# A hybrid block on one core: other projections beside the recurrence and the attention, and keys and values in seven-product sets

## The chip, the core and the metric

The kernel runs on one core of one Trainium2 chip. Its engines are TensorE (PE in the profile; PEld is its weight load), VectorE (DVE), ScalarE (ACT), GpSimd (POOL) and SyncE (SP). They run at the same time and wait for each other through semaphores. DMAs are issued from SP (weights) and from POOL (most else). The metric is the device time of one execution in microseconds (us), the median of the runs.

## The reference

256 tokens and 256 context tokens of width 2048 go through one block in float32. After a modulated norm, one wide projection `w_in` gives all inputs of an attention branch and of a recurrent branch (HGRN2, both directions, 16 heads of 128). Both are gated, projected and merged.

```python
xn = rmsnorm(h, norm_gain[l]) * (1.0 + scale) + shift
cn = rmsnorm(hc, norm_gain[l]) * (1.0 + scale_c) + shift_c
aq, ak, av, ag, hq, hff, hfb, hi, hg, ma, mb = split_columns(xn @ w_in[l])
caq, cak, cav, cag, chq, chff, chfb, chi, chg, cma, cmb = split_columns(cn @ w_in[l])
...
att_branch = window_attention(q, k, v, k_c, v_c, sink_logits[l]) * jax.nn.silu(ag)
...
o, _, _ = hgrn2_bidir(q_h, v_h, k_f, g_f, k_b, g_b, s_f, s_b)
hg_branch = hgrn_readout(o, hgrn_norm_gain[l], hg)
...
y_a = hg_branch @ w_o_hgrn_l
y_b = att_branch @ w_o_attn_l
y = jax.nn.sigmoid(m_a + b_m[0]) * y_a + jax.nn.sigmoid(m_b + b_m[1]) * y_b
return y @ w_out_l
```

The attention has 16 query heads and 4 key and value heads of 128, a rotary position (rope) on queries and keys, a window over the own tokens, all context tokens, and a sink. Context tokens are needed for keys, values, forget gates and the recurrent values; the other projections are of the own 256 tokens.

## The kernel before

**Numbers in two parts.** A float32 operand is kept as a high part and a low part, both float32r. `wchunk` (L69) loads a weight chunk of 128x1024 values through SP (tile `raw`, four buffers), ScalarE copies the high part (`wh`, L76) and VectorE subtracts it to get the low part (`wl`, L77). Each product is then three matmuls: high by high, low by high, high by low (`mm_high_first`, L87: L91, L92, L94). The activations lie in `xHL`: `xH` and `xL`, 16 blocks of 128 rows by 512 columns, of which columns 0 to 255 are the own tokens and 256 to 511 the context. The context half is called `XH`, `XL` once it is free.

**Projections.** `proj_tok_g` (L99) is a generator: it works through 8 chunks for a tile of 512 output columns, 24 matmuls of 512 columns a chunk for four token tiles and 12 for two, and yields after each chunk with the matmul columns it issued. `proj_col_x_g` (L138) does the same with features on the partitions. `STEP` is 24 x 512 columns. `quad_tok` (L657) computes 512 output columns for all 512 tokens by a seven-product scheme (as Strassen's, with combinations of the weights formed on VectorE and sums of the activations formed once, in `S`), in two halves of the depth, 24 matmuls of 256 columns a product. `quad_col` (L609) is its counterpart for the forget gates.

**Order of the stages.** Modulation and norm; the recurrent values, by `quad_tok` but for the first; the forget gates, by `quad_col`; the recurrence in 8 pairs of heads (`pair`, L766); `part_a` (L1166: recurrent branch times `w_oh`); the attention (`attend`, L1255); `part_b` (L1337: attention branch times `w_oa`); the output projection.

**How work is woven.** In the quad stage, the recurrence and the attention, TensorE's order is the written one (`manual_schedule`); a planner orders the other engines by its own simulation and by priorities, the pairs' and the attention's steps highest, weight splits next, all else after. `pair` yields the number of STEPs of filler that its next step should have behind it; `weave` (L1013) then draws on a filler generator until so much has been issued. The filler is `side_work` (L1097) for `SIDE[n]` yields, then the query projection of the next pair. `with_gates` (L1125) puts a chunk of the modulation gate (w_ada, on VectorE, `gates`) between, once in 3 STEP. `alternate` (L1029) takes one step of `attend` and one of `fill`. Each of the 32 heads by token tiles n has two steps in `attend`: `scores(n)` with the softmax, and `turned(n-2)`, the four transposes of the probabilities, with `values` once in four tiles.

**What fills what.** The side work holds the output gates of the recurrence, six of the eight merge gates, and the projections of keys and values (`attn_keys`, `attn_values`). The attention's filler `fill` holds queries and gates of the head groups 1 to 3 (`group_in`) and two merge gates. The queries and gates of group 0 are woven with the key transposes ahead of the attention, and `part_a` stands alone between recurrence and attention, with up to 16 steps of the modulation gate in it.

**Buffers.** "sm" is a ring of three tiles of 128x512 that all small results share, "bb" one of two. PSUM has four banks for projections (`pj`) and one each under the names `tp`, `o`, `al1`, `al2`. Results that wait for a later stage go to DRAM tiles and back through POOL's queue (`v_dr`, `hg_dr`, `ma_dr`, `mb_dr`, `k_dr`).

Of the kernel before, what the change touches and what calls it, by code (L numbers as in the profile page):

```python
# [14 lines left out]
P = 128  # L15
# [23 lines left out]
def block_kernel(ctx: ExitStack, tc: tile.TileContext, x, c, cx, c_ctx, w_ada, b_ada, norm_gain, w_in,  # L39
# [184 lines left out]
    k_dr = dram.tile([P, 2048], F32, name="k_dr")  # L224
# [309 lines left out]
    with pl("sp", reuse_waits="tile") as sp:  # L534
# [179 lines left out]
        with tc.manual_schedule(engines={mybir.EngineType.PE}):  # L714
# [17 lines left out]
    biases = {}  # L732
# [33 lines left out]
    def pair(g, p, grp, F, banks_q):  # L766
# [140 lines left out]
        yield 1.5  # L907
# [21 lines left out]
        yield 1.5  # L929
# [9 lines left out]
        yield 3.0  # L939
# [14 lines left out]
        yield 1.0  # L954
# [14 lines left out]
        yield 1.0  # L969
# [59 lines left out]
    def alternate(g, filler, n):  # L1029
        for _ in g:  # L1030
            for _ in range(n):
                next(filler, None)
        run(filler)

# [20 lines left out]
    def rope(dst, src, t):  # L1055

        cos = cs[:, K_COS + t * HD: K_COS + (t + 1) * HD].unsqueeze(1).to_broadcast([P, 4, HD])
        dve.tensor_tensor(dst, src.rearrange("p (h d) -> p h d", h=4), cos, op=ALU.mult)
# [6 lines left out]
        tf = tmp.rearrange("p h a s d -> p h (a s d)")  # L1065
# [8 lines left out]
    def attn_keys():  # L1074
        bk = yield from proj_tok_g(w_in, C_K, x_st, range(4))
        for t in range(4):
            kr_ = base.tile([P, 512], F32, tag="sm", name="kr", bufs=3)
            if t < 2:
                rope(kr_.rearrange("p (h d) -> p h d", h=4), bk[t], t)
            else:  # L1080
                act.activation(kr_, bk[t], AF.Copy)
            nc.gpsimd.dma_start(k_dr[:, t * 512: (t + 1) * 512], kr_)

    def attn_values():
        bv = yield from proj_tok_g(w_in, C_V, x_st, range(4))
        for t in range(4):
            rows = slice(8 + 2 * t, 10 + 2 * t)
            split(XH[:, rows, :], XL[:, rows, :], bv[t].rearrange("p (r c) -> p r c", r=2))
# [7 lines left out]

    def side_work():  # L1097
        for step in ((output_gate(1), merge_out(0, 0), output_gate(2)), (attn_keys(),),
                     (merge_out(0, 1), output_gate(3), merge_out(0, 2)),
                     (merge_out(0, 3), merge_out(1, 2), merge_out(1, 3)), (attn_values(),)):  # L1100
            for g in step:
                yield from g
                yield 0

    side = side_work()
    SIDE = (13, 14, 9, 13, 14, 13, 14, 9)

    def inputs(n, res):

        units, F = 0, None  # L1110
        for _ in range(SIDE[n]):
            got = next(side, None)
            if got is None:
                break
            units += got
            if F is None and n < 7 and units >= 4 * STEP:
                F = load_forgets(n + 1)
            yield got
# [17 lines left out]
    def merge_gate(bm, n, row, dst):  # L1136
        bb = biases.pop((row, n), None)
        if bb is None:
            bb = bias_row(row, n)
        for t in range(2):  # L1140
            dve.tensor_tensor(dst[:, t, :], bm[t], bb, op=ALU.add)
            act.activation(dst[:, t, :], dst[:, t, :], AF.Sigmoid)
# [23 lines left out]
    def part_a(n):  # L1166
        by = proj_tok_g(w_oh, n * 512, b_st, range(2))
        for z in range(4):
            take(gate, 1)
            for _ in range(2):  # L1170
                next(by)
        by = result(by)
        for t in range(2):
            dve.tensor_tensor(y[n][:, t, :], by[t], y[n][:, t, :], op=ALU.mult)

    for n in range(4):
        y[n] = hp.tile([P, 2, 512], F32, tag="vc", name="y") if n == 3 else \
            fp.tile([P, 2, 512], F32, tag="F0" if n < 2 else "F1", name="y", bufs=2 if n < 2 else 1)
        nc.gpsimd.dma_start(y[n].rearrange("p t c -> p (t c)"), ma_dr[n])
    for n in range(4):  # L1180
        part_a(n)
# [19 lines left out]
    with tc.manual_schedule(engines={mybir.EngineType.PE}):  # L1201
# [4 lines left out]
        kr = at.tile([P, 4, 4, HD], F32, tag="A", name="kr")  # L1206
        nc.gpsimd.dma_start(kr.rearrange("p t h d -> p (t h d)"), k_dr)

        def keys():
            for z in range(2):  # L1210
                tks = [ps.tile([P, 512], F32, tag=tg, name="tkk") for tg in ("tp", "o")]
                for t in range(2):
                    for j in range(4):
                        pe.transpose(tks[t][:, j * P: (j + 1) * P], kr[:, 2 * z + t, j, :], ident)

                for t in range(2):
                    dst = [X[:, z: 8: 2, t * P: (t + 1) * P] for X in (XH, XL)]
                    split(dst[0], dst[1], tks[t].rearrange("p (j t) -> p j t", j=4))
                yield

        def group_in(j, st):

            bq = yield from proj_tok_g(w_in, C_Q + 512 * j, x_st, range(2))
            def turn_q(t):
                qr = base.tile([P, 4, HD], F32, tag="bb", name="qr", bufs=2)
                rope(qr, bq[t], t)
                yield
                tk = ps.tile([P, 512], F32, tag="o", name="tkq")
                for i in range(4):
                    pe.transpose(tk[:, i * P: (i + 1) * P], qr[:, i, :], ident)  # L1230
                qh, ql = [X[:, t].rearrange("p h t -> p (h t)") for X in st["q"]]
                with tc.high_priority(2 * PRIO):
                    act.activation(qh, tk, AF.Copy, scale=HD ** -0.5)
                    dve.scalar_tensor_tensor(ql, tk, HD ** -0.5, qh.bitcast(F32), op0=ALU.mult, op1=ALU.subtract)

            turning = [turn_q(t) for t in range(2)]
            next(turning[0])
            st["q"] = [at.tile([P, 2, 4, P], F32R, tag=tg, name="qTa") for tg in Q_TAGS[j % 2]]
            st["g"] = gt_tile(j, [P, 4, T], "ga")
            for hf in range(2):  # L1240
                bg = proj_col_x_g(w_in, C_G + 512 * j + 256 * hf)
                for k0 in range(0, KT, 4):
                    next(bg)
                    yield
                    if (hf, k0) == (0, 0):
                        next(turning[1])
                    if hf == 0 and k0 in (4, 12):
                        next(turning[k0 // 8], None)
                for i, b in enumerate(result(bg)):
                    gs = halves_sum(b, "bb", 2)  # L1250
                    gi = st["g"][:, 2 * hf + i, :]
                    act.activation(gi, gs, AF.Sigmoid)
                    dve.tensor_tensor(gi, gi, gs, op=ALU.mult)
# [240 lines left out]
```

## Time and profile before

| | us |
|---|---|
| median of the runs (1612.27 to 1616.04) | 1614.99 |
| the profiled execution | 1614.37 |
| its span | 1612.6 |
| busy TensorE, VectorE, ScalarE, GpSimd | 1579.2, 1152.4, 863.7, 84.8 |
| quad stage, from the recurrent values on | 200 to 573 |
| recurrence | 573 to 1052 |
| `part_a` up to the last of it | to about 1140 |
| attention with its first projections | 1140 to 1440 |

The page is of one execution. Busy times are of instructions, and matmuls overlap, so the start of one matmul to the start of the next tells more than the length of one. A row of windows gives, for a stretch, its length and then busy time and number of instructions of PE, PEld, DVE, ACT and POOL, the granted TensorE clock (1.00 is full), the busy share of the DMA engines and GB/s. A row of waits gives who waited at which line, for whom, the sum in us, how often, and the longest.

### The profile page before, as it was taken

Reading aid. Unit: us, or ns where it says so; the run is one execution under the profiler, and the core shown is the slowest. Engines: PE = TensorE matmul, PEld = TensorE weight load, DVE = VectorE, ACT = ScalarE, POOL = GpSimd, SP = SyncE. Lnnn points to the kernel's source line nnn. Section 1 sums busy time; section 2 is a strip of 40 time slices with the busy share of each in tenths; the row PEclk is TensorE's granted clock in tenths of the full one; section 3 lists DMA queues with packets and bytes.
Section 4 is the critical chain, followed back from the end, with each engine's and each line's share of the span. In section 5 each row is a group of like instructions: output and inputs, shape, how many; then the busy total and the mean of one; then the engine's idle time right before and its main releaser. Section 6 shows DMA issues by size and latency. Waiting matters only on the chain. (4 is left out here: it accounts for less than half of the span.)

```text
span 1612.6 us, 26672 instructions
## 1 busy us (share of the span) xinstructions
PE 1579.2 (98%) x10522; PEld 1336.6 (83%) x10522; DVE 1152.4 (71%) x1703; ACT 863.7 (54%) x1337; POOL 84.8 (5%) x183
## 2 busy tenths in 40 slices
PE   7999999999999999999999999999999999999998
PEld 4567899988888887888888888878888888888887
DVE  4449777788888877876888787556567767756674
ACT  4334443356565565655666666434457677744442
POOL 2000000000000010111111010000000000000000
PEclk9999999999999999999999999999999999999999
DMA  9995434444444486564767766467554445467662
GB/s 364 386 373 170 157 131 131 131 132 131 131 135 140 133 276 217 191 223 158 228 224 240 244 213 205 159 215 249 180 179 144 146 141 164 158 230 235 207 208 80
DMA packets 230013, 312.76 MB, mean 194 GB/s; under 512 B 10080, under 2 KB 145664, under 8 KB 228992
## 3 DMA queue, kind: packets, MB, share of 16 engines
q1 hardware_dynamic: 216800, 266.85, 50.7%
q0 software_dynamic: 12368, 43.11, 7.7%
q8 instruction: 82, 1.34, 0.3%
q10 hardware_dynamic: 720, 1.11, 0.2%
q14 instruction: 43, 0.35, 0.1%
HBM read 290.05 MB, written 20.98 MB: 193 GB/s over the span
## 5 line engine op out<-in xcount | busy, mean ns | idle before, releaser
L77 DVE TENSOR_TENSOR wl<-raw,wh 128x1024 fp32r<-128x1024 f32 x308 | 374.5, 1222 | 171.7 <-ACT wh L76 157.4
L76 ACT ACTIVATE wh<-raw 128x1024 fp32r<-128x1024 f32 x308 | 324.2, 1059 | 303.9 <-PE pj L92 186.8
L91 PE MATMUL pj<-wh,xHL 128*128 128x512 f32 (+1 forms) x832 | 325.0, 392 | 1.5 <-DVE hsum L156 0.8
L92 PE MATMUL pj<-wh,xHL 128*128 128x512 f32 (+1 forms) x832 | 319.8, 386 | 0.0
L94 PE MATMUL pj<-wl,xHL 128*128 128x512 f32 (+1 forms) x832 | 215.1, 386 | 0.1
L91 PEld LDWEIGHTS pj<-wh,xHL 128*128 128x128 f32 x832 | 156.4, 188 | 33.7 <-ACT sg L211 1.9
L92 PEld LDWEIGHTS pj<-wh,xHL 128*128 128x128 f32 x832 | 156.5, 188 | 29.7
L94 PEld LDWEIGHTS pj<-wl,xHL 128*128 128x128 f32 x832 | 154.2, 188 | 32.0 <-DVE wl L77 0.5
L145 PE MATMUL pj<-xHL,wh 128*128 128x512 f32 x512 | 131.0, 397 | 0.0
L605 ACT ACTIVATE wh<-raw 128x1024 fp32r<-128x1024 f32 x76 | 80.4, 1058 | 77.0 <-PE pj L704 21.0
L606 DVE TENSOR_TENSOR wl<-raw,wh 128x1024 fp32r<-128x1024 f32 x76 | 92.9, 1222 | 34.3 <-ACT wh L605 34.1
L145 PEld LDWEIGHTS pj<-xHL,wh 128*128 128x128 f32 x512 | 92.6, 188 | 17.3
L91 PE MATMUL pj<-wh,bH 128*128 128x512 f32 x256 | 101.1, 396 | 4.2 <-ACT wh L76 3.5
L605 ACT ACTIVATE wh<-T 128x1024 fp32r<-128x1024 f32 x57 | 60.5, 1061 | 82.0 <-DVE T L586 20.7
L92 PE MATMUL pj<-wh,bL 128*128 128x512 f32 x256 | 100.2, 393 | 0.0
L606 DVE TENSOR_TENSOR wl<-T,wh 128x1024 fp32r<-128x1024 f32 x57 | 69.6, 1221 | 20.1 <-ACT wh L605 19.9
L148 PEld LDWEIGHTS pj<-xHL,wl 128*128 128x128 f32 x512 | 69.8, 190 | 5.1
L148 PE MATMUL pj<-xHL,wl 128*128 128x256 f32 x512 | 71.3, 282 | 0.0
L94 PE MATMUL pj<-wl,bH 128*128 128x512 f32 x256 | 71.0, 393 | 0.1
L196 DVE SCALAR_TENSOR_TENSOR acc<-raw,cg,acc 128x512 f32<-128x512 f32 x60 | 45.0, 750 | 29.8 <-DMA raw<-in_w_ada_dram 29.4
L887 DVE TENSOR_TENSOR A<-A,X 128x512 f32<-128x512 f32 x96 | 61.9, 687 | 4.2 <-ACT F L814 2.8
L91 PEld LDWEIGHTS pj<-wh,bH 128*128 128x128 f32 x256 | 48.4, 189 | 15.4 <-ACT wh L76 4.5
(356 smaller groups left out, 2766.5 us busy)
## 6 DMA issues: line engine op xcount, KB each, us to landing
raw<-in_w_in_dram SPq DMA_DIRECT2D x300, 512.0 KB, 4.0
raw<-in_w_ada_dram SPq DMA_DIRECT2D x96, 512.0 KB, 7.8
raw<-in_w_o_hgrn_dram SPq DMA_DIRECT2D x32, 512.0 KB, 4.8
raw<-in_w_o_attn_dram SPq DMA_DIRECT2D x32, 512.0 KB, 4.3
F<-F POOLq DMA_DIRECT2D x29, 512.0 KB, 5.5
raw<-in_w_out_dram SPq DMA_DIRECT2D x28, 512.0 KB, 4.2
v<-vo POOLq DMA_DIRECT2D x8, 512.0 KB, 2.9
X<-in_x_dram SPq DMA_DIRECT2D x2, 1024.0 KB, 7.2
```

The source lines that it names most:

```text
L76: act.activation(h[:, :n], raw[:, :n], AF.Copy)
L77: dve.tensor_tensor(lo[:, :n], raw[:, :n], h[:, :n].bitcast(F32), op=ALU.subtract)
L91: pe.matmul(o, s[0], m[0], start=first, stop=False)
L92: pe.matmul(o, s[1], m[0], start=False, stop=False)
L94: pe.matmul(o, s[0], m[1], start=False, stop=last)
L145: pe.matmul(o.rearrange("p (a t) -> p a t", a=2), h[:, j, cs_], xHL[:, :, k0 + j, :T], start=k0 + j == 0, stop=False)
L148: pe.matmul(o[:, :T], lo[:, j, cs_], xH[:, k0 + j, :T], start=False, stop=k0 + j == KT - 1)
L196: dve.scalar_tensor_tensor(acc, wr[:, j, :], cc, acc, op0=ALU.mult, op1=ALU.add)
L605: act.activation(h, src, AF.Copy)
L606: dve.tensor_tensor(lo, src, h.bitcast(F32), op=ALU.subtract)
L887: dve.tensor_tensor(av, av, f.unsqueeze(3).to_broadcast([P, 2, n2, b]), op=ALU.mult)
```

## The change

Keys and values are computed in the quad stage by `quad_tok` and stored in `kv_dr`. In the recurrence they are loaded from there: `attn_keys` ropes and transposes the keys, `attn_values` splits the values, both into the free context half of `xHL`. The side work takes all four query projections (`attn_queries`: rope, transposes, split, store to `q_dr`), all four gate projections of the attention (`attn_gates`, stored to `ag_dr`) and the two remaining merge gates. The transposes of a query tile are put into the list `late` and issued after the second and fourth chunk of the next block. `pair` asks for more filler (10.75 STEP instead of 8.5), and a gate chunk comes once in 2.6 STEP. The attention loads queries and gates of a group from DRAM, and its filler is `part_a`, one chunk for each head and token tile; its result goes to `xH`, `xL` (columns 0 to 255) instead of `bH`, `bL`, which `part_a` still reads. The merge gates of `part_b` all come from `mb_dr`.

```diff
+            for i, co in enumerate((C_K, C_V)):
+                quad_tok(co, kv_dr[i])
...
-        yield 1.5
+        yield 2.0
...
-        yield 1.5
+        yield 1.75
...
-        yield 3.0
+        yield 4.0
...
-        yield 1.0
+        yield 1.25
...
-        yield 1.0
+        yield 1.25
...
     def attn_keys():
-        bk = yield from proj_tok_g(w_in, C_K, x_st, range(4))
+        for z in range(2):
+            for t in range(2):
+                kr = base.tile([P, 512], F32, tag="sm", name="kr", bufs=3)
+                nc.gpsimd.dma_start(kr, kv_dr[0][t][:, z * 512: (z + 1) * 512])
+                if z == 0:
+                    kx, kr = kr, base.tile([P, 512], F32, tag="sm", name="kx", bufs=3)
+                    rope(kr.rearrange("p (r h d) -> p r h d", r=2, h=2), kx, t)
+                yield
+                tk = ps.tile([P, 512], F32, tag="tp", name="tkk")
+                for j in range(4):
+                    pe.transpose(tk[:, j * P: (j + 1) * P], kr[:, j * HD: (j + 1) * HD], ident)
+                dst = [X[:, z: 8: 2, t * P: (t + 1) * P] for X in (XH, XL)]
+                split(dst[0], dst[1], tk.rearrange("p (j t) -> p j t", j=4))
+                yield
...
+        bq = yield from proj_tok_g(w_in, C_Q + 512 * j, x_st, range(2))
+        for t in range(2):
+            qr = base.tile([P, 512], F32, tag="sm", name="qr", bufs=3)
+            rope(qr.rearrange("p (r h d) -> p r h d", r=2, h=2), bq[t], t)
+            late.append(lambda t=t, qr=qr: turn_q(t, qr))
+
+    def attn_gates(j):
+        for hf in range(2):
+            bg = yield from proj_col_x_g(w_in, C_G + 512 * j + 256 * hf)
+            for i, b in enumerate(bg):
+                gs = halves_sum(b, "bb", 2)
+                sg = base.tile([P, 512], F32, tag="sm", name="sga", bufs=3)[:, :T]
+                act.activation(sg, gs, AF.Sigmoid)
+                dve.tensor_tensor(sg, sg, gs, op=ALU.mult)
+                c0 = (2 * hf + i) * T
+                nc.gpsimd.dma_start(ag_dr[j][:, c0: c0 + T], sg)
...
+    late = []
+
     def side_work():
...
+        keys, values = attn_keys(), attn_values()
+        blocks = (output_gate(1), merge_out(0, 0), output_gate(2), attn_queries(0), merge_out(0, 1), output_gate(3),
+                  attn_queries(1), merge_out(0, 2), attn_gates(0), merge_out(0, 3), attn_queries(2), merge_out(1, 0),
+                  attn_gates(1), merge_out(1, 1), attn_queries(3), merge_out(1, 2), attn_gates(2), merge_out(1, 3),
+                  attn_gates(3))
+        for n, g in enumerate(blocks):
+            for k, got in enumerate(g):
+                yield got
+                if late and k in (1, 3):
+                    late.pop(0)()
+                elif n < 2:
+                    next(keys, None)
+                elif n > 16 and k % 2:
+                    next(values, None)
+            yield 0
...
-    SIDE = (13, 14, 9, 13, 14, 13, 14, 9)
+    SIDE = (20, 20, 20, 20, 20, 20, 20, 31)
...
-            if count[0] >= 3 * STEP:
-                count[0] -= 3 * STEP
+            if count[0] >= 2.6 * STEP:
+                count[0] -= 2.6 * STEP
...
     def part_a(n):
...
+        by = yield from proj_tok_g(w_oh, n * 512, b_st, range(2))
         for t in range(2):
             dve.tensor_tensor(y[n][:, t, :], by[t], y[n][:, t, :], op=ALU.mult)
...
+        yield
...
-                split(bH[:, hs, t * P: (t + 1) * P], bL[:, hs, t * P: (t + 1) * P], br)
+                split(xH[:, hs, t * P: (t + 1) * P], xL[:, hs, t * P: (t + 1) * P], br)
...
             for n in range(35):
+                if n in (8, 16):
+                    load_queries(n // 8 + 1, sts[n // 8 + 1])
+                if n in (11, 19):
+                    load_gates(n // 8 + 1, sts[n // 8 + 1])
...
+        def fill():
+            for n in range(4):
+                yield from part_a(n)
...
+        filler = fill()
+        for i, _ in enumerate(attend(sts)):
+            if i % 2 == 0:
+                next(filler, None)
+        run(filler)
...
     def part_b(n):
-        by = proj_tok(w_oa, n * 512, b_st, range(2))
+        by = proj_tok(w_oa, n * 512, x_st, range(2))
```

More of the change, by code (lines that the diff above doesn't have):

```diff
@@ L1166, in part_a @@
     def part_a(n):
[L1167 to L1172, printed above, removed]
+        by = yield from proj_tok_g(w_oh, n * 512, b_st, range(2))
         for t in range(2):
             dve.tensor_tensor(y[n][:, t, :], by[t], y[n][:, t, :], op=ALU.mult)
[L1176 to L1181, printed above, removed]
+        yield
     run(gate)
@@ L1204, in block_kernel, with load_queries @@
         nc.gpsimd.dma_start(sk, row_bcast(sink, 16))
[L1206 to L1209 removed]
+        def load_queries(j, st):
+            st["q"] = [at.tile([P, 2, 4, P], F32R, tag=tg, name="qTa") for tg in Q_TAGS[j % 2]]
             for z in range(2):
[L1211 to L1219, printed above, removed]
```

125 lines of the change are left out of this document (42 added, 83 removed).

## The prediction

> **What bounds the kernel now.** I read the page first (its table of busy time), then the windows by stage, then TensorE's waits, then the order of time at the places that matter.
>
> ```profile
> span 1612.6 us, 26672 instructions
> PE 1579.2 (98%) x10522; PEld 1336.6 (83%) x10522; DVE 1152.4 (71%) x1703; ACT 863.7 (54%) x1337; POOL 84.8 (5%) x183
> ```
>
> TensorE is busy for all but 1612.6 - 1579.2 = 33.4 us. So a gain can come from three places only: fewer matmuls, fewer idle gaps, or matmuls that run faster. The windows say where the gaps are.
>
> ```profile
> 0.00:20.00 20.00, 10.44 (x66) 9.52 (x66) 11.81 (x37) 12.34 (x27) 7.43 (x22) 1.00 0.94 342
> 573.00:1048.00 475.00, 465.39 (x4338) 396.45 (x4338) 365.65 (x617) 283.07 (x533) 49.83 (x112) 0.99 0.65 214
> 1060.00:1140.00 80.00, 76.52 (x335) 62.23 (x334) 50.79 (x56) 30.81 (x31) 0.58 (x1) 0.98 0.71 236
> 1198.00:1440.00 242.00, 242.00 (x1231) 204.44 (x1230) 173.33 (x321) 166.29 (x275) 2.16 (x4) 1.00 0.49 158
> 1527.00:1613.00 86.00, 77.72 (x434) 68.12 (x432) 46.10 (x64) 31.01 (x43) 1.12 (x2) 0.98 0.44 148
> ```
>
> Each row is a stretch, its length, then busy time of PE, PEld, DVE, ACT and POOL, the granted clock, the DMA share and GB/s. The start (9.6 us idle) and the end (8.3 us) are not touched. The recurrence (573 to 1048) has 9.6 us of idle, `part_a` (1060 to 1140) 3.5 us, and the attention (1198 to 1440) none at all. TensorE's waits name these gaps (total, times, longest):
>
> ```profile
> PE ob L981 <- DVE X L967: 5.8, 3, 3.2
> PE pj L91 <- ACT wh L76: 3.5, 2, 3.0
> ...
> PE kt L947 <- DVE A L887: 0.9, 2, 0.7
> ...
> PE al L962 <- ACT X L853: 0.8, 1, 0.8
> PE pj L91 <- DVE hsum L156: 0.8, 1, 0.8
> PE pj L91 <- DVE xHL L1072: 0.7, 1, 0.7
> ...
> PE tw L904 <- DVE F L764: 0.5, 1, 0.5
> ```
>
> They add up to 13.0 us. A long gap costs more than itself: after the 3.03 us wait in `part_a`, matmuls of 512 columns start 0.42 us apart for 3.9 us before they are back at 0.23.
>
> ```profile
> 1072.69 0.50 PE L91 MATMUL pj<-wh,bH 128*128 128x512 f32 x1 [3.03 <-ACT wh L76]
> ...
> 1073.26 0.62 PE L91 MATMUL pj<-wh,bH 128*128 128x512 f32 x1
> 1073.68 0.63 PE L92 MATMUL pj<-wh,bL 128*128 128x512 f32 x1
> ...
> 1077.15 0.39 PE L91 MATMUL pj<-wh,bH 128*128 128x512 f32 x1
> ```
>
> That is half speed for 3.9 us, so about 1.9 us lost. The two recurrence stretches that hold an L981 wait of over 2 us show the same in their clock:
>
> ```profile
> 640.00:700.00 60.00, 57.73 (x546) 49.89 (x545) 51.12 (x86) 39.08 (x74) 5.97 (x16) 0.97 0.65 217
> 940.00:1000.00 60.00, 56.84 (x534) 48.79 (x533) 48.98 (x84) 36.19 (x69) 4.96 (x10) 0.97 0.67 222
> ```
>
> A clock of 0.97 over 60 us is 1.8 us each. Gaps and slow clock together: 13.0 + 1.9 + 1.8 + 1.8 = 18.5 us. No re-ordering can win more than this.
>
> **The change part by part.**
>
> *Keys and values as seven-product sets.* Before, each is 8 chunks of 24 matmuls of 512 columns (L91, L92, L94) among the recurrence's fillers. After, each is one more `quad_tok`, of which three run now: 14 products of 24 matmuls of 256 columns.
>
> ```profile
> 140.13 0.39 PE L91 MATMUL pj<-wh,xHL 128*128 128x512 f32 x1
> ...
> 145.57 0.39 PE L91 MATMUL pj<-wh,xHL 128*128 128x512 f32 x1
> ...
> 203.17 0.28 PE L702 MATMUL pj<-wh,S 128*128 128x256 f32 x1
> ...
> 206.05 0.28 PE L702 MATMUL pj<-wh,S 128*128 128x256 f32 x1
> ```
>
> These are starts of neighbouring chunks: 145.57 - 140.13 = 5.44 us for 24 matmuls (0.227 each), 206.05 - 203.17 = 2.88 us for 24 (0.120 each). So 8 x 5.44 = 43.5 us become 14 x 2.88 = 40.3 us: 3.2 us less for each projection, **6.4 us** for both. The window of the second `quad_tok` confirms it, and that nothing else ends later there:
>
> ```profile
> 241.00:281.00 40.00, 40.00 (x336) 40.00 (x335) 30.15 (x30) 15.82 (x16) 1.07 (x2) 1.00 0.40 130
> ```
>
> TensorE has no gap although VectorE does 30 us of combinations and splits in it. PEld is busy for all 40 us: half the columns do not take half the time, because each 256-column matmul needs its own weight load. The Trainium skill ("TensorE: Matmul & The Clock Gate", section "Back-to-back issue gap") gives an isolated gap of N/2.4 + 2.5 ns, which is 109 ns at 256 columns; by that, an estimate, a projection would take 336 x 0.109 = 36.7 us and the saving would be about 13.7 us. The trace's 0.120 decides against it.
>
> *Moved fillers.* In units of 24 matmuls of 512 columns (STEP, 5.44 us), counted from the yields: the recurrence's side list had 52 units and gets 76; the attention had 32 beside it and 8 ahead of it, and gets the 16 of `part_a`, which stood alone. 52 + 40 + 16 = 108 become 76 + 16 = 92, and the missing 16 are keys and values. The transposes (16 of keys, 32 of queries) stay in number. The query and gate halves are the same instructions in another place. So TensorE's work changes by the 6.4 us only, and the rest of the sum is gaps.
>
> *`part_a` as filler.* Its 3.5 us wait for weights came where GEMM chunks ran alone at 2.72 us apiece beside gate loads and y loads; beside the attention a chunk has about 4.7 us, and the gate chunks come earlier, in the recurrence (2.6 STEP apart instead of 3). I take the wait and its slow clock as gone: **-5.4 us**.
>
> *The recurrence.* A pair now asks for 10.75 STEP of filler instead of 8.5, 12 us more. The phase ahead of L981, where 5.8 of the 9.5 us are lost, grows from 1.0 to 1.25 STEP (5.4 to 6.8 us), and the one where VectorE builds the levels from 3 to 4 STEP. Gaps and clock here are 9.5 + 3.6 = 13.1 us. Both ends: all gone (0), or as many per us in a stage that is a fifth longer (16). The longest L981 wait, 3.2 us, isn't covered by 1.4 us more, the other two (2.3 and 0.4) nearly; I take 8, **-5.1 us**. VectorE's share stays: 365.65 of 475 is 77%; 4.5 more chunks a pair at 1.22 us and some 6 us of rope, gates and splits make about 58 of 72 us, 80%.
>
> *New waits in the recurrence.* TensorE's order there is the written one, and twelve new groups of transposes (4 of keys, 8 of queries) are put into it. Everything behind such a group waits with it. A key block is loaded by POOL one chunk (2.72 us) ahead of its transposes, and two of the four go through `rope` first.
>
> ```profile
> F<-F POOLq DMA_DIRECT2D x29, 512.0 KB, 5.5
> ...
> L1058 DVE TENSOR_TENSOR kr<-pj,cs 128x512 f32<-128x512 f32 x2 | 1.4, 686 | 5.0 <-PE pj L94 5.0
> ...
> L1063 DVE TENSOR_TENSOR rt<-pj,cs 128x256 f32<-128x256 f32 x4 | 1.5, 414 | 0.0
> ...
> L1066 DVE TENSOR_TENSOR kr<-kr,rt 128x512 f32<-128x512 f32 x2 | 1.4, 684 | 0.0
> ...
> POOL F L1093 <- PE al L841: 82.0, 7, 20.2
> ```
>
> `rope` is 0.69 + 2 x 0.41 + 0.68 = 2.2 us. If a load starts only where it is written, a key with rope is late by 5.5 + 2.2 - 2.72 = 5.0 us and one without by 2.8: 15.6 us for four. The last row speaks against that: POOL's loads of F stand at the head of its queue for 12 us on average before their buffer is free, so loads are placed as early as their buffer allows, and a key's buffer ("sm", three of them) is free at the start of a pair. For queries the cover is two chunks, 5.4 us, against rope (2.2 us, or 4.4 for the second) on a VectorE that is busy 80% of the time: bounds 0 and about 8 x 2 us. I take 4 us for all twelve, near the lower end: **+4 us**. The 44 or so further DMA issues on POOL in the recurrence (q, ag, keys, values) have the 90% of POOL that is idle.
>
> *The attention with half the filler.* A head and token tile has two filler chunks today, and one after: scores(n), chunk, transposes(n-2), scores(n+1). From scores(n) to its transposes lie three chunks, two transposes and two scores: 3 x 2.72 + 2 x 0.4 + 2 x 0.7 = 10.4 us. What must fit in it:
>
> ```profile
> 1297.26 0.39 PE L85 MATMUL sc<-xHL,qTa 128*128 128x512 f32 x1
> ...
> 1300.48 0.67 ACT L1271 ACTIVATE pr<-sc,mx 128x512 f32<-128x512 f32 x1
> ...
> 1303.72 0.71 ACT L1275 ACTIVATE pr<-pr,mx 128x512 f32<-128x512 f32 x1
> ```
>
> From the end of the scores (1297.65) to the end of the scaling (1304.43) it takes 6.8 us. So it fits, with 3.6 us to spare. VectorE and ScalarE become denser:
>
> ```profile
> L77 DVE TENSOR_TENSOR wl<-raw,wh 128x1024 fp32r<-128x1024 f32 x67 | 82.0, 1224 | 40.7 <-ACT wh L76 40.6
> ...
> L76 ACT ACTIVATE wh<-raw 128x1024 fp32r<-128x1024 f32 x66 | 69.8, 1057 | 58.0 <-PE pj L92 36.0 <-PE pj L145 21.9
> ```
>
> Without their 67 chunk splits they do 173.3 - 82.0 = 91 and 166.3 - 69.8 = 96 us in the stretch; with 32 splits (39 and 34 us) both come to 130 us, still with the query and gate work that leaves. TensorE does 242 - 67 x 2.72 = 60 us of its own there, and 87 us of `part_a`: about 150 with the ends. It stays the bound, at 87% for the others at most. But the generator of `part_a` yields a ninth time, for the product with y, without a matmul: at n = 8, 17 and 26 no chunk covers the step, and the cover falls to 7.7 us (at n = 26 values(5) comes right behind the scores). Bounds: 0, and, if the chain grows to 12 us in the denser queues, (12 - 10.4) / 3 = 0.5 us a step, 17 us. I take a little over 1 us at each of the three thin steps: **+4 us**. The seam itself is covered: the last pair has 31 side steps (some 13.5 STEP for its 10.75), so some 15 us of chunks run while the first queries (v and qk buffers) come in, against 5.5 us for such a load.
>
> **Sum**, from the profiled execution (1614.37 us with 1.8 us around the span; the median of the runs is 1614.99): 1614.4 - 6.4 - 5.4 - 5.1 + 4 + 4 = **1605.5 us**.
>
> **The rivals.**
>
> *Every gap is covered.* The longer phases and the thin attention hold without a wait: 1614.4 - 6.4 - 18.5 = 1589.5 at best, about 1596 with 6 us left. For it: two stretches of the recurrence have no gap even now, and the attention none. Against: VectorE's queue is as full as before. Chance 0.12.
>
> *The saving is eaten.* New waits equal the old ones plus 6.4 us: 1612 to 1618, about 1614. For it: 80% and 87% loads beside a TensorE that follows a written order. Chance 0.19.
>
> *Transposes late in TensorE's order (slower).* Keys wait for their loads (15.6 us by the working above), and every wait near 3 us adds 1.9 us of slow clock (four: some 7 us): 1605.5 - 4 + 15.6 + 7 = 1624. It decides from the point where a key's load is issued later than about 5 us ahead of its transposes, or a query's rope ends over 5.4 us after its projection. The Trainium skill ("TensorE: Matmul & The Clock Gate", "Step-by-step: what each phase is for") says that matmuls stay in program order and only weight loads are pulled ahead, so nothing passes a late transpose; the trace agrees, with no matmul begun in the 3.03 us wait above. Chance 0.10.
>
> *The softmax chain exceeds its cover (slower).* 17 us instead of 4: 1618.5, more with the clock. It needs the chain to grow from 6.8 to 12 us. Chance 0.08.
>
> **How the numbers follow.** My forecast (1600 to 1611.5) has 0.51. A measurement of this kernel can tell about 0.2%, 3.2 us, from no change: faster is below 1611.8, slower above 1618.2. Faster 0.51 + 0.12 = 0.63, same 0.19, slower 0.18. The range 1594 to 1620 leaves out the best of the first rival and most of the two slow ones, some 0.15 to 0.2.
>
> **What would show it.** Right: five windows like the 241 to 281 one, with L702 over 0.120 us apart; the recurrence near 580 us with under 10 us idle; an attention of about 150 us with gaps at n = 8, 17 and 26 only; no wait on L76 in `part_a`. Wrong: a TensorE wait on `tkk` or `tkq`, or on the groups just behind them, of several us (late keys or queries); waits on `tkp` spread over all 32 steps (the chain); a clock under 0.97 in a stage.

## The result: 1.6% slower, and the profile after

| | before | after |
|---|---|---|
| median of the runs, us | 1615.51 (1612.27 to 1620.53) | 1642.07 (1637.35 to 1642.90) |
| ratio to before, 95% interval | | 1.0156 [1.0123, 1.0188] |
| span of the profiled execution, us | 1612.6 | 1640.6 |

The forecast was 1605.5 us (1594 to 1620). The kernel is slower, and outside the range. In the page after, the first line is the span, the second the busy time of each engine.

```profile
span 1640.6 us, 27474 instructions
PE 1583.8 (97%) x10810; PEld 1349.9 (82%) x10810; DVE 1186.4 (72%) x1745; ACT 856.5 (52%) x1338; POOL 116.5 (7%) x240
```

TensorE now idles for 1640.6 - 1583.8 = 56.8 us, where it was 33.4. Busy time should have fallen by the 6.4 us of the seven-product sets, and rose by 4.6: part of it runs at a lower clock, and a slow matmul counts as busy. The windows by stage say where. Columns: stretch, length, busy PE, PEld, DVE, ACT, POOL, granted clock, DMA share, GB/s.

```profile
200.00:402.00 202.00, 202.00 (x1683) 201.91 (x1682) 154.41 (x149) 79.88 (x83) 5.89 (x11) 1.00 0.41 134
653.00:1290.00 637.00, 606.45 (x5064) 514.43 (x5063) 484.65 (x780) 362.07 (x645) 77.24 (x161) 0.98 0.71 234
1300.00:1455.00 155.00, 149.27 (x702) 122.16 (x701) 110.85 (x247) 105.04 (x203) 5.85 (x11) 0.98 0.49 152
653.00:720.00 67.00, 61.55 (x417) 51.39 (x416) 52.26 (x83) 36.34 (x55) 7.05 (x21) 0.95 0.70 236
720.00:800.00 80.00, 77.19 (x623) 64.78 (x622) 60.89 (x97) 45.40 (x80) 6.07 (x14) 0.98 0.70 228
880.00:960.00 80.00, 71.87 (x502) 61.66 (x500) 58.05 (x95) 44.24 (x80) 7.89 (x16) 0.96 0.64 209
1120.00:1200.00 80.00, 71.89 (x587) 60.12 (x586) 59.23 (x96) 41.70 (x75) 8.97 (x18) 0.94 0.67 217
```

The first row holds five `quad_tok`: from the first matmul at 199.77 to the first of the next stage at 401.36, 40.3 us each, without a gap. The second is the recurrence with its 76 units of filler: 30.6 us idle, where the shorter one had 9.6. The third is the attention: 5.7 us idle, where it had none. The last four are the parts of the recurrence with a clock under 1.00: 0.05 x 67 + 0.02 x 80 + 0.04 x 80 + 0.06 x 80 = 13.0 us lost beside the gaps, where it was 3.6. TensorE's waits in the recurrence after (who waited, for whom; sum in us, times, longest) give the gaps names:

```profile
PE tkq L1099 <- DVE bL L1007: 6.8, 1, 6.8
PE tkq L1099 <- DVE qr L1062: 6.3, 2, 4.6
PE pj L94 <- DVE wl L77: 4.0, 2, 2.3
PE tkk L1081 <- DVE kx L1062: 3.6, 1, 3.6
PE al L964 <- ACT Kmt L952: 2.8, 3, 1.4
PE to L1001 <- DVE xHL L1107: 2.4, 1, 2.4
PE tw L906 <- DVE F L766: 1.9, 1, 1.9
PE ob L981 <- DVE redg L204: 1.8, 1, 1.8
```

Of the old waits, the 5.8 us for `X` (L981 before, L983 after) are gone; the row of L981 here is another matmul, which finds bank `o` still held by the end of the gate. New are the waits of the transposes of the moved projections, `tkq` (queries, 13.1 us) and `tkk` (keys, 3.6), and of `to`, which finds the bank that a query block still holds (2.4). These 19.1 us are the new waits; the other 11.5 us stand where 9.6 were. The attention waits at its three thin steps only (n = 8, 17 and 26):

```profile
PE tkp L1276 <- DVE pT L1068: 4.2, 2, 2.1
PE oba L84 <- DVE pT L1068: 0.9, 1, 0.9
PE oba L83 <- ACT pT L1067: 0.6, 1, 0.6
```

How a query comes late is seen on VectorE after, in order of time (start, us, line, operation):

```profile
1158.80 0.97 DVE L858 COPY_PREDICATED X<-mk,al 128x128 f32<-128x128 uint8 x3
1164.96 0.75 DVE L196 SCALAR_TENSOR_TENSOR acc<-raw,cg,acc 128x512 f32<-128x512 f32 x1 [5.20 <-DMA raw<-in_w_ada_dram]
...
1175.07 0.68 DVE L1054 TENSOR_TENSOR qr<-pj,cs 128x512 f32<-128x512 f32 x1
...
1178.73 1.29 DVE L889 TENSOR_TENSOR A<-A,X 128x512 f32<-128x512 f32 x2
1179.93 0.68 DVE L1062 TENSOR_TENSOR qr<-qr,rt 128x512 f32<-128x512 f32 x1
```

and on TensorE in the same stretch:

```profile
1169.35 1.21 PE L94 MATMUL pj<-wl,xHL 128*128 128x512 f32 x4 [1.69 <-DVE wl L77]
...
1180.76 1.09 PE L1099 MATMUL tkq<-cs,qr 128*128 128x128 f32 x4 [4.57 <-DVE qr L1062]
```

VectorE stood idle for 5.2 us ahead of a gate operation (L196) whose weights had not landed; what came behind it then ran without a pause. Weight splits, decays, levels and rope then queued up. The projection's last matmuls had ended at about 1170.6; the first rope operation of the query began at 1175.07, the last one that its transposes need ended at 1180.6, and TensorE, in written order, stood for 4.57 us. So rope took 5.5 us for four operations that last 2.2 us together, because the rope of the second tile, a weight split and a level operation ran between them. In the other three query blocks the first rope took 5.5, 5.5 and 4.3 us in the same way.

The longest wait (6.8) is of another kind. TensorE, then the last read of VectorE from the bank:

```profile
910.10 0.60 PE L1001 MATMUL to<-cs,so 128*128 128x128 f32 x4
917.48 1.09 PE L1099 MATMUL tkq<-cs,qr 128*128 128x128 f32 x4 [6.78 <-DVE bL L1007]
...
916.86 0.47 DVE L1007 SCALAR_TENSOR_TENSOR bL<-to,cols,bH 128x256 fp32r<-128x256 f32 x1
```

`tkq` stands right behind the pair's own output transposes `to` and asks for the same bank, `tp`; VectorE had not yet read the low part `bL` from it (L1007).

### The profile page after: what moved, and what is told of

Its sections match the earlier page's. It is cut to its first block, busy times and chain, and to the rows that moved or that the text cites. A ratio compares the mean times of both kernels' runs of the same rounds, so it can differ in the third digit from the quotient of the medians.

```text
span 1640.6 us, 27474 instructions
## 1 busy us (share of the span) xinstructions
PE 1583.8 (97%) x10810; PEld 1349.9 (82%) x10810; DVE 1186.4 (72%) x1745; ACT 856.5 (52%) x1338; POOL 116.5 (7%) x240
## 4 chain that ended last, share of the span: by engine, by line
PE 79%; DVE 7%; DMA 7%; issue 4%; ACT 2%; POOL 0%; SPq 0%; DVEq 0%; POOLq 0%; ACTq 0%
PE pj L91 10%; PE pj L92 10%; PE pj L94 10%; PE pm L632 5%; PE pj L632 5%; PE pj L145 5%; DMA raw<-in_w_ada_dram 3%; DVE wl L77 3%; PE pm L635 3%; PE pj L635 2%; PE pj L148 2%; PE pj L709 2%; PE pj L706 2%; PE pj L704 2%; PE pm L709 2%
## 5 line engine op out<-in xcount | busy, mean ns | idle before, releaser
L76 ACT ACTIVATE wh<-raw 128x1024 fp32r<-128x1024 f32 x292 | 306.0, 1058 | 251.0 <-PE pj L92 157.2
L94 PE MATMUL pj<-wl,xHL 128*128 128x512 f32 (+1 forms) x832 | 221.2, 390 | 4.5 <-DVE wl L77 4.5
L91 PEld LDWEIGHTS pj<-wh,xHL 128*128 128x128 f32 x832 | 158.7, 191 | 33.5 <-ACT sg L211 1.9
L92 PEld LDWEIGHTS pj<-wh,xHL 128*128 128x128 f32 x832 | 158.7, 191 | 30.4
L607 ACT ACTIVATE wh<-T 128x1024 fp32r<-128x1024 f32 x69 | 73.2, 1061 | 108.3 <-DVE T L588 31.3
L608 DVE TENSOR_TENSOR wl<-T,wh 128x1024 fp32r<-128x1024 f32 x69 | 84.2, 1220 | 26.8 <-ACT wh L607 26.8
L196 DVE SCALAR_TENSOR_TENSOR acc<-raw,cg,acc 128x512 f32<-128x512 f32 x60 | 44.8, 747 | 40.2 <-DMA raw<-in_w_ada_dram 39.9
L588 DVE TENSOR_TENSOR T<-raw,T 128x1024 f32<-128x1024 f32 x46 | 56.2, 1222 | 1.0
L632 PE MATMUL pm<-S,wh 128*128 128x512 f32 x224 | 56.1, 392 | 0.0
L706 PE MATMUL pj<-wh,S 128*128 128x256 f32 x208 | 51.0, 283 | 0.0
L704 PE MATMUL pj<-wh,S 128*128 128x256 f32 x208 | 51.0, 283 | 0.0
```

The source lines that it names most:

```text
L76: act.activation(h[:, :n], raw[:, :n], AF.Copy)
L91: pe.matmul(o, s[0], m[0], start=first, stop=False)
L92: pe.matmul(o, s[1], m[0], start=False, stop=False)
L94: pe.matmul(o, s[0], m[1], start=False, stop=last)
L607: act.activation(h, src, AF.Copy)
L608: dve.tensor_tensor(lo, src, h.bitcast(F32), op=ALU.subtract)
```

## The experiments

A ratio is to the kernel before on the same chip, with its 95% interval; a change from one experiment to another is the quotient of two ratios, in us at 1642.07 unless said.

**Give rope the highest priority in the planner.**

```diff
-            rope(qr.rearrange("p (r h d) -> p r h d", r=2, h=2), bq[t], t)
+            with tc.high_priority(2 * PRIO):
+                rope(qr.rearrange("p (r h d) -> p r h d", r=2, h=2), bq[t], t)
...
-                    late.pop(0)()
+                    with tc.high_priority(2 * PRIO):
+                        late.pop(0)()
```

(and the same around the rope and split of the keys)

> The changed kernel, with rope, transposes' evacuation and split of the side work's keys and queries in the highest planner priority instead of the lowest; nothing else. Theory A (the new transposes come too early for results that VectorE does last): TensorE's waits on tkk and tkq (16.7 us of 30 us of gaps in the recurrence) and on tp behind them (2.4) fall under 5 us, and the slow clock behind them with them; 1642 becomes about 1622. Theory B (VectorE is full while the levels are built; whatever is put first, something else is late): the tkk and tkq waits go, but waits on weight low parts (L94), the levels (al) or ob take their place; 1635 to 1645.

1644.95 us, 1.0163 [1.0134, 1.0192]: no change. Of TensorE's waits, with this edit:

```profile
PE tkq L1101 <- DVE qr L1062: 6.9, 2, 4.0
PE tkq L1101 <- DVE bL L1007: 6.8, 1, 6.8
```

Neither expectation came: a priority moves nothing here. VectorE's order is planned from simulated times, and if in those the rope is in time, a higher priority has nothing to push forward (the reason is argued; that nothing moves is measured).

**Issue the query transposes two chunks later.**

```diff
-                if late and k in (1, 3):
+                if late and k in (3, 5):
```

> The changed kernel, with the query transposes issued after the fourth and sixth chunk of the next block instead of the second and fourth (10.9 us of cover instead of 5.4). Theory A: the tkq waits (13.1 us in three places, followed by slow clock) are gone, key waits (3.6) stay; about 1642 - 13 - 6 = 1623. Theory B: the order of VectorE is the same and only TensorE's place changes, so the gaps shrink too, but by less than half (the full stretch is longer than 5.4 us); 1633 to 1640.

1628.80 us, 1.0071 [1.0047, 1.0096]: 0.84% less than after, 13.7 us, between the two expectations in time and with the first in the query waits. Of its waits in the recurrence, these two belong to the transposes:

```profile
PE tkk L1081 <- DVE kx L1062: 5.0, 1, 5.0
...
PE tkq L1099 <- issue: 1.8, 1, 1.8
```

The query waits fell from 13.1 us to 3.2 (another of 1.4 is in smaller rows), about 10 us. Since other waits grew, the keys' among them, the gaps of the recurrence fell by 6.9 us in all, to 23.7; its slow clock fell by 6.4, from 13.0 to 0.05 x 67 + 0.04 x 80 = 6.6 us. The keys were left as they were, and wait on.

**Take out the empty step of `part_a`.**

```diff
             dve.tensor_tensor(y[n][:, t, :], by[t], y[n][:, t, :], op=ALU.mult)
-        yield
```

> The changed kernel, with the ninth yield of part_a taken out, so that each of the first 32 steps of the attention has a chunk of filler. If the thin steps n = 8, 17 and 26 make the attention's gaps: tkp and oba waits (5.7 us) fall under 1 us, clock 1.00 in the attention, 1642 becomes about 1634. If the cover of one chunk is too thin in general: gaps of the same sum stay, spread over other steps, 1640 to 1644.

1633.56 us, 1.0101 [1.0077, 1.0125]: 0.54% less, 8.9 us. The window of the attention:

```profile
1290.00:1460.00 170.00, 170.00 (x825) 141.07 (x824) 124.48 (x265) 117.02 (x217) 7.90 (x15) 1.00 0.56 171
```

No gap and full clock: the ninth yield without a matmul was the attention's whole loss, 5.7 us of gaps and 0.02 x 155 = 3.1 us of clock.

**Keys and values without the seven products.**

```diff
-                quad_tok(co, kv_dr[i])
+                bv0 = proj_tok(w_in, co, x_st, range(4))
+                for t in range(2):
+                    vo = fp.tile([P, 2, 512], F32, tag="F0", name="vo", bufs=2)
+                    with tc.high_priority(2 * PRIO):
+                        act.activation(vo[:, 0, :], bv0[t], AF.Copy)
+                        dve.tensor_copy(vo[:, 1, :], bv0[2 + t])
+                    nc.gpsimd.dma_start(kv_dr[i][t], vo.rearrange("p a c -> p (a c)"))
```

> The changed kernel, with keys and values at the same place by the plain projection of 192 matmuls of 512 columns instead of the seven-product set; stored and loaded the same. If the set is worth its difference of matmul time (2 x 3.2 us) whatever follows: 1642 + 6.4 = 1648.5, up to 1651 with the evacuation of the four banks between the two. If its extra work on VectorE (22 combinations and splits of 1.22 us instead of 8) costs it something later: 1642 to 1646.

1649.03 us, 1.0199 [1.0171, 1.0226]: 0.42% more, 7 us. The intervals leave room for 0 to 14; with the 40.3 us of a set in the window above against 43.5, the 6.4 us stand.

**Another PSUM bank for the transposes (`o` in place of `tp`).**

```diff
-            tk = ps.tile([P, 512], F32, tag="tp", name="tkq")
+            tk = ps.tile([P, 512], F32, tag="o", name="tkq")
```

(and the same for `tkk`)

> The changed kernel, with the transposes of keys and queries in the PSUM bank o instead of tp, which the pairs' own transposes (to) use. Theory C (the bank tp is the trouble: 6.8 us of tkq behind bL and 2.4 us of to behind the query's low part): these 9.2 us and the slow clock behind them go; about 1642 - 9 - 4 = 1629. Theory A: the place is late whatever the bank; the waits stay or move to o (sb, kt, ob share it); 1638 to 1645.

1653.02 us, 1.0228 [1.0204, 1.0251]: slower still. The waits of its queries:

```profile
PE tkq L1099 <- DVE qr L1062: 8.6, 3, 4.6
PE tkq L1099 <- DVE so L993: 7.3, 2, 4.0
PE tkq L1099 <- ACT Kmt L952: 3.6, 1, 3.6
```

Bank `o` is held by the pair as well, so the wait on `bL` became others. Rope's waits stay (8.6 us), so the shared bank alone is not the cause. What a bank of their own would give the transposes was not tried.

**No gate weights loaded.** The products of the gate read a constant tile.

```diff
-        wr = wload(w_ada, k0 * P, 2, (4096 + 512 * g,), 512)[1][:, 0]
+        wr = cs[:, :512].unsqueeze(1).to_broadcast([P, 2, 512])
```

> The changed kernel, with the modulation gate's 32 chunks of w_ada (16 MB) not loaded: VectorE's products read a constant tile instead; this part of the result is left out. Theory D (VectorE, in order, stands before the gate's product until its DMA has landed, 39.9 us in 20 places, and is late for all that is queued behind): the waits on tkq, L94 and al fall by more than half, about 1642 - 18 = 1624. Theory A (the cover of the new transposes is too short in any case): tkq waits stay near 13 us, 1636 to 1642.

1628.86 us, 1.0078 [1.0062, 1.0095]: 0.77% less, 12.6 us. Of its waits in the recurrence:

```profile
PE tkq L1099 <- DVE bL L1007: 5.5, 1, 5.5
PE tkq L1099 <- DVE qr L1062: 5.4, 2, 3.1
PE tkk L1081 <- DVE kx L1062: 3.0, 1, 3.0
```

A second cause, then, between the two expectations: the waits of `al` (2.8 us) are gone and all gaps of the recurrence fell by 9.3 us, but 10.9 of the 13.1 us on `tkq` remain. At the place shown above the query still waits, 3.1 us instead of 4.6, and rope takes 5.5 us (1166.69 to 1172.2) although VectorE no longer stands idle ahead of it: the transposes still stand too near.

**A gate chunk once in 3 STEP, as before** (2.6 to 3 in two lines of `with_gates`).

> The changed kernel, with a gate chunk once in 3 STEP as before, not in 2.6. Theory D: fewer gate chunks in the recurrence, 30 instead of 34, so a little less of VectorE's waits: 1634 to 1640, with the last chunks at the seam to the attention (up to 5 us of gap there). Theory A: 1640 to 1645; the places change by chance.

1651.49 us, 1.0216 [1.0188, 1.0244]: slower by 0.6%, a miss. The gate did not end within the recurrence and waited at its end (2.2 us for `tgr`, 2.1 for `tqg`), while `tkq` kept 14.4 us in all. VectorE's waits for gate weights were 50.6 us instead of 39.9, not less as expected.

**Three edits together:** transposes at `k in (3, 5)`, no empty step, keys at every second chunk.

```diff
-                elif n < 2:
+                elif n < 2 and k % 2:
                     next(keys, None)
```

> The changed kernel with three edits of distance together: query transposes after the fourth and sixth chunk, a key step after every second chunk instead of every chunk, and no ninth yield in part_a. If the parts add (13.2 and 8.5 us from the runs of the first two alone, 5.0 us of tkk wait and about 2 of clock for the keys): 1642 - 13 - 8.5 - 7 = 1613.5, level with the kernel before. If the key waits only move: 1618 to 1622.

1612.86 us (10 runs), 0.9986 [0.9970, 1.0002]: level with the kernel before, 1.67% (27.5 us) under after. Later queries and no empty step give 13.7 + 8.9 = 22.6, so the keys are worth about 5 (they were not tried alone). Recurrence and attention now:

```profile
653.00:1290.00 637.00, 620.00 (x5169) 526.11 (x5168) 496.20 (x806) 380.28 (x670) 81.29 (x166) 0.99 0.73 241
1290.00:1460.00 170.00, 170.00 (x813) 140.55 (x813) 122.17 (x249) 109.25 (x203) 5.93 (x11) 1.00 0.56 179
```

17.0 us of gaps are left in the recurrence, no longer on one tile. Rope takes as long as before (5.5 us in three of the four query blocks), but now it is covered.

**Where the transposes stand, sooner and later.** After, with `k in (0, 2)`:

> The changed kernel, with query transposes after the first and third chunk of the next block instead of the second and fourth: 2.7 us of cover instead of 5.4, nothing else. Theory A: each of up to eight transposes may be up to 2.7 us later; tkq waits rise from 13 to 20 to 30 us, and the slow clock with them: 1642 + 12 to 1642 + 30. If the distance isn't what counts: 1638 to 1646.

1645.59 us, 1.0187 [1.0156, 1.0217]. As a total this is not told apart from after, which the first expectation missed; the wait for rope grew, from 6.3 us:

```profile
PE tkq L1099 <- DVE qr L1062: 17.4, 3, 7.3
```

The 6.8 us on `bL` and the 2.4 of `to`, both for bank `tp`, are not among its waits: all gaps of the recurrence are 33.1 us, where they were 30.6.

The three edits, with `k in (4, 7)` instead of `(3, 5)`:

> The kernel of the three edits, with query transposes after the fifth and eighth chunk of the next block instead of the fourth and sixth. Theory A: the last 3.8 us of tkq waits and 1.5 us of to behind it go, 1613 becomes about 1608. If a query block that is held longer in two of the three sm buffers holds up the pairs: new waits on tw, al or sb, 1613 or more.

1625.22 us, 1.0050 [1.0031, 1.0070]: 0.64% worse than `(3, 5)`.

```profile
PE tkq L1099 <- DVE bL L1007: 8.4, 2, 4.3
```

Later is not better without limit. These places meet the pair's own transposes on bank `tp`. Rope asks for distance, and the bank asks for the right place.

**What is left after the three edits.** VectorE's waits for gate weights in the recurrence: first the kernel before, then the one with three edits.

```profile
DVE acc L196 <- DMA raw<-in_w_ada_dram: 28.9, 16, 4.8
```

```profile
DVE acc L196 <- DMA raw<-in_w_ada_dram: 43.6, 22, 5.4
```

Per microsecond of recurrence that is the same (28.9 / 475 and 43.6 / 637, 6 to 7%); what changed is what stands behind it. Four runs ask what it costs. First, the three edits with the gate reading the constant tile, as above:

> The kernel of the three edits of distance, and the modulation gate's chunks of w_ada not loaded (its products read a constant tile; this part of the result is left out). Theory D as a second cause (VectorE stands 43.6 us before the gate's loads, and TensorE's waits on L94, al, tw and ob, 10.6 us, follow from it): most of these waits go, 1613 becomes about 1602. If they come from VectorE's plain load in the level phase: 1608 to 1613.

1597.22 us, 0.9879 [0.9857, 0.9901]: 1.07% less, 17 us. Then with every load still made, and only the products reading the constant:

```diff
-        wr = wload(w_ada, k0 * P, 2, (4096 + 512 * g,), 512)[1][:, 0]
+        wload(w_ada, k0 * P, 2, (4096 + 512 * g,), 512)
+        wr = cs[:, :512].unsqueeze(1).to_broadcast([P, 2, 512])
```

> The kernel of the three edits, with the gate's chunks of w_ada still loaded into the weight ring but read by nothing: the products read a constant tile (this part of the result is left out). If VectorE's wait for the loads is the cost: as without the loads, 1597 to 1601. If traffic and buffers are: 1609 to 1614.

1599.21 us, 0.9888 [0.9865, 0.9911]: 0.98% less. Its recurrence:

```profile
653.00:1290.00 637.00, 627.51 (x5231) 534.25 (x5231) 495.57 (x813) 391.21 (x690) 79.95 (x167) 1.00 0.74 243
```

The DMA share stays at 0.74 and the gain stays too. So it is not the traffic. What went with the loads is VectorE's wait in its order; but a load that nothing reads also gives its buffer of `raw` back as soon as it has landed, and this run does not separate the two. (9.5 us of gaps are left, and no slow clock.) Next, the products written two steps of the filler behind their load:

```diff
         wr = wload(w_ada, k0 * P, 2, (4096 + 512 * g,), 512)[1][:, 0]
+        yield
...
+            if wait[0]:
+                wait[0] -= 1
+                if wait[0] == 0:
+                    next(gate, None)
...
+                wait[0] = 2
```

> The kernel of the three edits, with the gate's product written two filler chunks behind its load, so that nothing is left out. Theory D: if the place in the text decides where VectorE's queue has the product, its waits of 43.6 us fall below 15 and 1613 becomes about 1605. If the planner puts it where it believes the load has landed, whatever the text: waits near 40 us and 1610 to 1616.

1620.92 us, 1.0019 [1.0006, 1.0032]: 0.33% (5 us) worse than without it; a new wait of 4.9 us for the end of the gate (`tgr`) is of that size. VectorE's wait is as it was:

```profile
DVE acc L197 <- DMA raw<-in_w_ada_dram: 44.6, 23, 5.1
```

Where it is written does not matter here; that the planner places the products by its own times, in which the load is sooner done, is argued. What is left to try is a load that starts earlier. `raw` has only four buffers, shared with all weights, so the last run gives the gate its own: eight blocks of `XH` that are free in the recurrence until the values come, filled through POOL's queue a whole gate step ahead, with nothing left out:

```diff
+    def gate_load(i):
+        b = xHL[:, 0, 8 + 4 * (i % 2): 12 + 4 * (i % 2), T:]
+        for j in range(2):
+            r0 = (2 * (i % 8) + j) * P
+            src = w_ada[r0: r0 + P, 4096 + 512 * (i // 8): 4608 + 512 * (i // 8)]
+            nc.gpsimd.dma_start(b[:, 2 * j: 2 * j + 2, :], src.rearrange("p (r c) -> p r c", r=2))
+        return b
...
+        b = gate_load(0)
+        for i in range(32):
+            b, ahead = (gate_load(i + 1) if i < 31 else None), b
+            gate_chunk(accT[:, 0, :], i, ahead)
...
-            if count[0] >= 2.6 * STEP:
-                count[0] -= 2.6 * STEP
+            if count[0] >= 2.35 * STEP:
+                count[0] -= 2.35 * STEP
```

> The kernel of the three edits, with the gate's chunks loaded by POOL into two buffers of their own (the free context half of xH, blocks 8 to 15, until the values come), each a whole gate step ahead of its product, once in 2.35 STEP so that all are done before the values are loaded; nothing left out. If the wait is the cost and the early load removes it: VectorE's waits on w_ada under 10 us, 1598 to 1604. If POOL's queue holds the loads up behind its other waits: 1606 to 1616.

1608.77 us, 0.9951 [0.9932, 0.9969]: 0.5% (8 us) under the kernel before and 2% under after. The time came as in the second expectation. Its waits on the gate's weights, on VectorE:

```profile
DVE acc L206 <- DMA xHL<-in_w_ada_dram: 12.3, 7, 3.0
```

and the largest of TensorE's in the recurrence:

```profile
PE to L1013 <- DVE so L1005: 4.5, 1, 4.5
```

Over two thirds of the waits went, and a third of the gain of the 17 us came, although the gate no longer takes buffers from `raw`. The largest wait left has POOL behind it in part: `so` needs `ss`, whose two operations on POOL run at 823.73 and 830.81 (L181, L182), with issues of gate loads and query stores between them. But `ss` is done at 832.1 and `so` begins at 837.21, after other work of VectorE. How much of the missing gain POOL's queue holds was not tried.

## Why the prediction was wrong, step by step

Forecast beside measurement, in us of the profiled execution:

| step | forecast | measured |
|---|---|---|
| two seven-product sets | -6.4 | -6.4 (windows, plain sets 7 slower) |
| wait and clock in `part_a` | -5.4 | -5.4 (no wait on L76 is left, 3.5; the 1.9 of clock is the forecast's own; not isolated) |
| recurrence, old and new waits together | -5.1 + 4 | +21.0 gaps, +9.4 clock |
| attention at the thin steps | +4 | +5.7 gaps, +3.1 clock |
| sum | -8.9 | +27.4 (span: +28.0) |

- **The step that failed** is "I take 4 us for all twelve" groups of transposes. They took 19.1 us of waits, and most of the 9.4 us of clock came behind them: moving eight of them by two chunks gave 13.7 us, and spreading the keys about 5 more. With both, the recurrence has 13.6 us less of gaps (30.6 to 17.0) and 8.2 us less of slow clock (13.0 to 0.02 x 80 + 0.04 x 80 = 4.8). The bounds had the size (15.6 for the keys, 16 for the queries), and I took the lower end of both; slow clock behind these waits was put at nothing. "A TensorE wait on `tkk` or `tkq`" was the sign named for being wrong, and it showed.
- **Why the lower end was wrong.** For queries, the cover of 5.4 us was set against 2.2 or 4.4 us of rope on an engine "busy 80% of the time" (it was 484.65 / 637 = 76%). The mean says nothing about the order. From its first to its last operation the first rope of a block took 4.3 to 5.5 us, not 2.2, so most or all of the 5.4 us of cover was gone even before any delay. What had piled up during a 5.2 us wait of VectorE came on top; with that wait away the same query was still 3.1 us late. The waits for gate weights were in the trace of before, 28.9 us of them in 16 pieces, and the prediction made no use of them.
- **The rival came for another reason.** "Transposes late in TensorE's order" is what happened, at a chance of 0.10 and 1624 us. For keys I had weighed the load; it was issued 7.5 us ahead of the transposes (669.41 to 676.9), earlier than the 5 us that the rival named, and rope on VectorE, 5.0 us instead of 2.2, made the first one late (`kx`, 3.6 us). For queries rope made two of the three waits (6.3 us), and the bank `tp` the longest (6.8), which the prediction did not name.
- **The old gaps** did not give their 5.1 us. `X` at L981, 5.8 us, is gone as said, but 4.0 us on `wl` and 2.8 on `Kmt` came, and the gaps beside the new transposes are 11.5 us where they were 9.6. With the gate's weights out, `al` stopped waiting and `wl` fell to 1.9 us, so these too come in part from the late VectorE.
- **A sign that did not fit its own count.** "The recurrence near 580 us" left out most of the filler: 24 units more of 5.44 us are 131 us, so 475 us become 606 before any wait. Measured are 637: 606, 21.0 of gaps and 9.4 of clock.
- **The attention** was right in place: gaps at the thin steps and nowhere else. It was not right in what waits there. The forecast set the softmax chain against a thinner cover; but at n = 8 the probabilities had been scaled by 1325.1, and the transposes ran at 1332.10. They waited for bank `tp`, which VectorE read late (`pT`), behind the product with y and a weight split; at n = 26 `values` waited for the split of the transposes just ahead of it. That the sum of the gaps (5.7 for 4) was near is luck. The size, 8.8 for 4, also lacked the clock, which the forecast had counted for a wait near 3 us only.
- **The softmax chain** did not exceed its cover: none of these waits is for it, and without the empty step there is no gap at all.

What stays open: which part of the 9.4 us of clock goes with which wait; how the 16 to 17 us that the gate's weights cost divide between VectorE's waits and the buffers of `raw`; and how much of them can be had without holding up POOL.

## What to carry to other kernels

A piece put into a written order on the engine that bounds the kernel needs cover against the worst queue of the engine that feeds it, not against its mean load, and against the time from the first to the last operation of its producer in that engine's order (here 5.5 us), not against the sum of their lengths (2.2): read that engine's own order and waits first, since a wait for a DMA in the middle of its order delays everything behind it although the engine looks a quarter idle. If the place can be chosen, try it on both sides; here two chunks later gave 14 us, and one or two more took 10 back, because of a shared bank. A filler generator that yields without issuing work leaves a hole in the cover, and the hole costs its clock as well.

## What the runs showed of the hardware that was not expected

Short gaps can bring the slow clock too. TensorE after, in order of time, at three waits:

```profile
669.17 0.66 PE L906 MATMUL tw<-cs,F 128*128 128x128 f32 x4 [1.86 <-DVE F L766]
670.48 0.63 PE L92 MATMUL pj<-wh,xHL 128*128 128x512 f32 x1
670.91 0.63 PE L91 MATMUL pj<-wh,xHL 128*128 128x512 f32 x1
...
1063.88 0.65 PE L1001 MATMUL to<-cs,so 128*128 128x128 f32 x4 [2.45 <-DVE xHL L1107]
1064.60 0.39 PE L92 MATMUL pj<-wh,xHL 128*128 128x512 f32 x1
1064.83 0.40 PE L91 MATMUL pj<-wh,xHL 128*128 128x512 f32 x1
...
1332.10 0.83 PE L1276 MATMUL tkp<-cs,pr 128*128 128x128 f32 x4 [2.10 <-DVE pT L1068]
...
1334.43 0.63 PE L92 MATMUL pj<-wh,bL 128*128 128x512 f32 x1
1334.86 0.63 PE L91 MATMUL pj<-wh,bH 128*128 128x512 f32 x1
```

After gaps of 1.86 and 2.10 us, matmuls start 0.43 us apart, half speed; after one of 2.45 us, 0.23 apart. So the length of a gap alone does not decide; what else does, where it falls in time perhaps, is not shown here. The Trainium skill ("TensorE: Matmul & The Clock Gate", "Why this matters for your kernels") tells to avoid idle gaps over about 3 us; these rows show slow clock after shorter ones, and the measurement decides. By these rows a gap of 2 us can cost nearly twice its length (some 3 us at half speed are 1.5 us more), and a sum over waits should carry a term for it.
